# A state-space mixer rewritten on tiles of TensorE's array, with its transfers and table loads moved

## The chip, the cores and the metric

The kernel runs on one core of one Trainium2 chip. The metric is the device time of one execution in microseconds (us), given as the median of several runs. Everything below in lines L1, L2, ... refers to the kernel before, unless it is said to be of the change.

## The reference

Two transformer blocks are computed for 256 tokens of width 1024 in float32. The second one is: FFN, S5 mixer, FFN, FFN, block attention, FFN. Only the S5 mixer concerns the change:

```python
def s5_mixer(h, w_in, ..., d_skip, w_glu, w_out):
    u = (h @ w_in).astype(f32)
    ...
    # u in 64 groups of 16 values, per group a complex state of 64
    # st[t] = lam * st[t-1] + bb @ u[t];  y[t] = Re(c @ st[t])
    y = ys... + d_skip.astype(f32) * u
    g = jax.nn.gelu(y)
    g = g * jax.nn.sigmoid(g @ w_glu.astype(f32))
    return g.astype(h.dtype) @ w_out
```

The comment lines stand for the scan of the reference, which runs over the tokens of a chunk. A state is linear in the inputs, so the kernel may cut the 256 tokens into 32 chunks of 8: within a chunk, an output is a sum over taps (a Toeplitz matrix in time), and from chunk to chunk only the state is carried.

## The kernel before

**Weights.** A class `Stream` brings weights in units of 128x1024 (512 KB). `Stream._fill` issues each unit's DMA from SP (L61) into one of four buffers `raw` (eight in the FFN), then makes a high part `wh` on ScalarE (L74) and a rest `wl` on VectorE (L75), since each product of two float32 values is made of three matmuls in a faster format. `Stream.next` hands out the next pair and starts the work for units further ahead: a `raw` buffer is refilled when its unit has been split, a pair `wh`, `wl` (two are there, four in the FFN) when the matmuls that read it are done. `mode_a` (L320) makes one tile of 128 outputs by 256 tokens out of one unit, in 24 matmuls: for each of eight k, `wh` by `xh` (L325), `wh` by `xl` (L326), `wl` by `xh` (L327). `split` makes the high and low parts of activations (L257 on ScalarE, L258 on VectorE).

**Order.** A scheduler orders each engine's instructions. From `u_tile(6)` on, `manual_schedule` fixes that of TensorE and VectorE as written, up to `in_order.close()`. SP's queue and ScalarE's stay the scheduler's.

**FFN.** 22 chunks of the hidden width; each chunk takes three units (gate, up, down). The first one (`l == 0`) stands right ahead of the mixer.

**Mixer** (`s5_mixer`, L1172 on), with tables made long before by `s5_prep`: `lam` (powers of lambda), `cw` and `me` (the output and input maps of a chunk), `kr` (the taps), `pr`, `pi` (powers over chunks).
1. `tap_weights` (L1193) writes the taps of each tile into block-diagonal matrices `s5kb`: odd tiles on ScalarE, eight copies each; even ones on GpSimd (L1200), one multiply each.
2. `u_tile` (L1206), eight times: `mode_a`, a scale by the norm (L1212), a write to `u_dram` (L1214). After tiles 3 and 7, eight DMAs (L1219) bring `u` back as `s5us`, with time inside the chunk on the partitions.
3. `contribution` (L1235), twice: 64 matmuls `s5eps` (L1244) of 64 rows of output by 32 chunks, on tiles of the array, and copies to `s5e` (L1246).
4. `taps` (L1226), eight times: eight matmuls `s5yps` (L1231), and a copy.
5. `chunks` (L1248) is the recurrence over the chunks for half of the groups, on VectorE: two blocks of 16 chunks run side by side, so 16 turns of four instructions (L1261 to L1264); then four instructions of 480 values (L1274 on) carry the end of the first block into the second.
6. `spread` (L1286) writes states into a block-diagonal layout `s5sbd`; `states_out` (L1297) makes 16 matmuls `s5sps` (L1302) per quarter, copies (L1307) and writes `y_dram`, five DMAs of eight on SP, three on GpSimd (L1310). `states_in` (L1313) reads it back with features on the partitions.
7. Sum of taps and states (L1367), Gelu (L1368), split; then the GLU: `mode_a` with `s5gps`, Sigmoid (L1376), multiply, split; then the output projection.

Of the kernel before, what the change touches and what calls it, by code (L numbers as in the profile page):

```python
# [35 lines left out]
class Stream:  # L36
# [59 lines left out]
    def next(self):  # L96
        i = self.pos
        self.pos += 1
        self._fill(*(i + sum(n for _, n in pools) for pools in (self.raw_pools, self.hl_pools)))
        if self.units[i][2]:  # L100
            return self.parts.pop(i)
        return self.raws.pop(i)
# [25 lines left out]
class Net:  # L128
# [5 lines left out]
    def __init__(self, ctx, tc, i, out, tap=None):  # L134
# [18 lines left out]
        self.v_order = [*range(self.NLO, P), *range(self.NLO)]  # L153
        self.ada_late = list(range(5, 5 + 8 * 5, 5))
# [165 lines left out]
    def mode_a(self, ps, w, xh, xl):  # L320

        wh, wl = w
        for k in range(KT):
# [598 lines left out]
    def ffn(self, l, last_deep=None, out=None):  # L922
        nc, tc = self.nc, self.tc
        with tc.tile_pool(name=f"ffn{l}", bufs=2) as fp:
# [5 lines left out]
            prev = row = None  # L930
            for c in range(NFF):
                if c == last_deep:
                    self.stream.shallow()
# [66 lines left out]
    def s5_prep(self, lo, hi):  # L1000
# [169 lines left out]
        self.s5 = (lam, cw, me, kr, grp, pr, pi)  # L1170

    def s5_mixer(self):  # L1172
        nc, tc, i = self.nc, self.tc, self.i
        Q = 32
        lam, cw, me, kr, grp, pr, pi = self.s5
        with ExitStack() as st:
            wp = st.enter_context(tc.tile_pool(name="s5w", bufs=1))
            dp = st.enter_context(tc.tile_pool(name="s5d", bufs=1, space=bass.MemoryType.DRAM))
            u_dram = dp.tile([64, 16, 8, Q], F32, name="u_dram")
            y_dram = dp.tile([64, 16, 8, Q], F32, name="y_dram")  # L1180
            xh, xl = self.gained(self.cols[:, self.MIX_G : self.MIX_G + KT])
            rx = self.rstd()
            row = None
            l8 = wp.tile([P, 2, 2, Q], F32, name="s5l8")
# [4 lines left out]
            kbs = {}  # L1189

            uT = wp.tile([P, KT, 8, Q], F32, tag="sA", name="s5uT")
            us = wp.tile([P, 64, Q], F32, tag="sB", name="s5us")
            def tap_weights(f):  # L1193
                kb = wp.tile([P, 8, 8, 16], F32, tag="s5kb", name="s5kb", bufs=5)
                k = kr[:, f].rearrange("p (k n) -> p k n", n=16)
                if f % 2:
                    for g in range(8):
                        nc.scalar.activation(kb[:, :, g], k, AF.Copy, scale=grp[:, g : g + 1])
                else:
                    nc.gpsimd.tensor_mul(kb, k.unsqueeze(2).to_broadcast([P, 8, 8, 16]),  # L1200
                                         grp[:, 0:8].unsqueeze(1).unsqueeze(3).to_broadcast([P, 8, 8, 16]))
                kbs[f] = kb

            for f in (0, 2):
                tap_weights(f)
            def u_tile(f):  # L1206
                nonlocal row
                ps = self.pm.tile([P, S], F32, tag="m", name="s5ups")
                self.mode_a(ps, self.stream.next(), xh, xl)
                if row is None:  # L1210
                    row = self.rstd_row(wp, rx)
                nc.vector.tensor_mul(uT[:, f], ps.rearrange("p (c s) -> p s c", s=8),  # L1212
                                     row.rearrange("p (c s) -> p s c", s=8))
                nc.sync.dma_start(u_dram[8 * f : 8 * f + 8].rearrange("g n s c -> (g n) (s c)"),  # L1214
                                  uT[:, f].rearrange("p s c -> p (s c)"))
                if f % 4 == 3:
                    gs = slice(8 * f - 24, 8 * f + 8)
                    for s in range(8):
                        nc.sync.dma_start(us[16 * s : 16 * s + 16, gs], u_dram[gs, :, s].rearrange("g n c -> n g c"))  # L1219

            yc = wp.tile([P, KT, S], F32, name="s5yc")
# [3 lines left out]

            def taps(f):  # L1226

                kb = kbs.pop(f)
                ps = self.pm.tile([P, S], F32, tag="m", name="s5yps")
                for k in range(8):  # L1230
# [55 lines left out]
            def spread(hf):  # L1286
                for half in range(2):
# [4 lines left out]
                    else:  # L1292
                        nc.scalar.activation(sbd[hf][hs, :, :, half], src, AF.Copy)

            ys = []

            def states_out(qt):  # L1297

# [360 lines left out]
```

## Time and profile before

| | before |
|---|---|
| median of 3 runs | 2112.12 us (2111.94, 2112.12, 2116.03) |
| profiled execution, its own time | 2112.87 us |
| its span | 2111.1 us |
| TensorE busy (PE) | 2013.5 us, 95% |
| weight loads (PEld) | 1750.2 us, 83% |
| VectorE busy (DVE) | 1532.5 us, 73% |
| ScalarE busy (ACT) | 1057.0 us, 50% |
| GpSimd busy (POOL) | 472.3 us, 22% |
| HBM traffic | 178 GB/s over the span |
| mean granted clock of TensorE | 0.984 |

The span runs from the first instruction to the last of the profiled execution; the execution's own time has 1.8 us around it. A busy share is an average over all stages: the mixer is a short part (from about 1267 us to the end of the output projection near 1400), in which the shares differ from these. In the profile's timelines each row gives the start, the busy time, the engine, the line, the operation with its output and inputs, how many instructions the row holds, and in brackets the idle time of the engine just before and what ended it.

### The profile page before, as it was taken

How to read it: one execution, taken by the hardware profiler on the slowest of the kernel's cores; microseconds unless marked ns; L12 is line 12 of the kernel's file. 1: busy time of each engine (PE TensorE's matmuls, PEld its weight loads, DVE VectorE, ACT ScalarE, POOL GpSimd, SP SyncE). 2: the span in 40 equal slices, each digit the busy share in tenths (PEclk: the TensorE clock that was granted, in tenths of full speed). 3: DMA queues.
4: the chain of work that ended last, by engine and by line, in shares of the span. 5: the costliest groups of instructions: out<-in, count | busy, mean ns of one | idle time of the engine just before them, and what ended most of it. 6: DMA issues, size and time to landing. Idle time of an engine off the chain costs nothing. (4 is left out here: it accounts for less than half of the span.)

```text
span 2111.1 us, 33643 instructions
## 1 busy us (share of the span) xinstructions
PE 2013.5 (95%) x12222; PEld 1750.2 (83%) x12222; DVE 1532.5 (73%) x2986; ACT 1057.0 (50%) x1761; POOL 472.3 (22%) x506
## 2 busy tenths in 40 slices
PE   7998999999999899999999998899999999999999
PEld 5777999999999677788878888788887888777887
DVE  5867489878988666998776667566667666776666
ACT  4564544443444445555555544455555555565554
POOL 0000003028999232000031111101111111210111
PEclk9999999999999999999999999899999999999999
DMA  8773455554444776455555534355554555444552
GB/s 334 235 273 122 138 181 172 173 180 153 150 151 156 265 256 233 174 189 187 181 174 189 189 129 131 90 177 183 190 189 160 190 190 190 141 140 146 188 188 97
DMA packets 129623, 378.59 MB, mean 179 GB/s; under 512 B 26897, under 2 KB 41281, under 8 KB 129330
## 3 DMA queue, kind: packets, MB, share of 16 engines
q1 hardware_dynamic: 128448, 373.76, 52.5%
q0 software_dynamic: 1008, 2.69, 0.4%
q8 instruction: 96, 1.57, 0.3%
q14 instruction: 69, 0.57, 0.1%
q10 hardware_dynamic: 2, 0.00, 0.0%
HBM read 366.96 MB, written 9.44 MB: 178 GB/s over the span
## 5 line engine op out<-in xcount | busy, mean ns | idle before, releaser
L75 DVE TENSOR_TENSOR wl<-raw,wh 128x1024 fp32r<-128x1024 f32 (+1 forms) x595 | 743.1, 1251 | 372.1 <-ACT wh L74 368.6
L74 ACT ACTIVATE wh<-raw 128x1024 fp32r<-128x1024 f32 (+1 forms) x628 | 662.6, 1056 | 585.6 <-issue 316.6
L325 PE MATMUL ups<-xh,wh 128*128 128x256 f32 x1024 | 292.1, 285 | 0.3 <-ACT act_lo L803 0.2
L326 PE MATMUL ups<-xl,wh 128*128 128x256 f32 x1024 | 288.9, 282 | 0.0
L327 PE MATMUL ups<-xh,wl 128*128 128x256 f32 x1024 | 288.7, 282 | 0.0
L948 POOL TENSOR_TENSOR sgl<-sgl,rrow 128x256 f32<-128x256 f32 x88 | 126.1, 1433 | 718.1 <-ACT sgl L947 718.1
L335 PE MATMUL gps<-xx,wh 128*128 128x512 f32 x704 | 253.9, 398 | 6.6 <-DVE xx L314 6.6
L335 PE MATMUL upps<-xx,wh 128*128 128x512 f32 x704 | 251.0, 395 | 0.0
L343 PE MATMUL acc<-wh,gl 128*128 128x512 f32 x512 | 202.9, 398 | 6.4 <-DVE gl L258 6.2
L341 PE MATMUL acc<-wh,gh 128*128 128x512 f32 x512 | 202.3, 396 | 4.5 <-ACT gh L257 2.3
L727 POOL TENSOR_SCALAR ob<-iota,idxT 128x128 f32<-128x128 f32 x256 | 195.9, 783 | 34.8 <-PE ups L327 32.2
L336 PE MATMUL gps<-xx,wl 128*128 128x256 f32 x704 | 198.1, 281 | 0.5 <-DVE wl L75 0.5
L336 PE MATMUL upps<-xx,wl 128*128 128x256 f32 x704 | 197.7, 281 | 0.0
L325 PEld LDWEIGHTS ups<-xh,wh 128*128 128x128 f32 x1024 | 194.6, 190 | 0.9 <-ACT act_lo L803 0.8
L327 PEld LDWEIGHTS ups<-xh,wl 128*128 128x128 f32 x1024 | 193.8, 189 | 0.1
L326 PEld LDWEIGHTS ups<-xl,wh 128*128 128x128 f32 x1024 | 193.6, 189 | 0.1
L335 PEld LDWEIGHTS gps<-xx,wh 128*128 128x128 f32 x704 | 133.3, 189 | 38.1 <-DVE xx L314 7.8
L335 PEld LDWEIGHTS upps<-xx,wh 128*128 128x128 f32 x704 | 132.2, 188 | 30.8
L342 PE MATMUL acc<-wl,gh 128*128 128x512 f32 x380 | 150.8, 397 | 0.8 <-DVE wl L75 0.8
L341 PE MATMUL acc<-wh,hh 128*128 128x512 f32 x352 | 139.1, 395 | 6.6 <-ACT hh L257 6.5
L342 PE MATMUL acc<-wl,hh 128*128 128x512 f32 x352 | 138.3, 393 | 0.0
L336 PEld LDWEIGHTS gps<-xx,wl 128*128 128x128 f32 x704 | 133.5, 190 | 4.4 <-DVE wl L75 0.9
(406 smaller groups left out, 3691.9 us busy)
## 6 DMA issues: line engine op xcount, KB each, us to landing
raw<-peer_u SPq DMA_DIRECT2D x128, 512.0 KB, 3.3
raw<-peer_v SPq DMA_DIRECT2D x128, 512.0 KB, 3.3
raw<-ffn_gate SPq DMA_DIRECT2D x88, 512.0 KB, 3.2
raw<-ffn_up SPq DMA_DIRECT2D x88, 512.0 KB, 3.2
raw<-ffn_down SPq DMA_DIRECT2D x88, 512.0 KB, 3.2
raw<-w_ada SPq DMA_DIRECT2D x28, 512.0 KB, 4.5
raw<-w_in SPq DMA_DIRECT2D x24, 512.0 KB, 6.4
raw<-moba_w_qkv SPq DMA_DIRECT2D x24, 512.0 KB, 3.2
```

What stands on the lines that cost most here:

```text
L74: nc.scalar.activation(h[:, :n], raw[:, :n], AF.Copy)
L75: nc.vector.tensor_sub(lo[:, :n], raw[:, :n], h[:, :n].bitcast(F32))
L325: self.nc.tensor.matmul(ps, wh[:, s], xh[:, k], start=(k == 0), stop=False)
L326: self.nc.tensor.matmul(ps, wh[:, s], xl[:, k], start=False, stop=False)
L327: self.nc.tensor.matmul(ps, wl[:, s], xh[:, k], start=False, stop=(k == KT - 1))
L335: self.nc.tensor.matmul(ps, wh[:, s], xx[:, k], start=(k == 0), stop=False)
L336: self.nc.tensor.matmul(ps[:, 0], wl[:, s], xx[:, k, 0], start=False, stop=(k == KT - 1))
L341: mm(acc, lh, wh, start=start, stop=False)
L342: mm(acc, lh, wl, start=False, stop=False)
L343: mm(acc, ll, wh, start=False, stop=stop)
L727: nc.gpsimd.tensor_scalar(b, iota, idx[:, 1, n : n + 1], None, ALU.is_equal)
L948: nc.gpsimd.tensor_mul(sg, sg, row)
```

## The change

- **Taps as a Toeplitz table.** A DRAM tile `toep` takes, for each of eight tiles, one fill with zeros and eight writes of shifted taps: `toeplitz_out` issues these 72 DMAs on SP during chunks 2 to about 13 of the first FFN. `load_taps` brings four tiles of 512 KB at a time back to SBUF, twice in the mixer. The GpSimd and ScalarE work of `tap_weights` goes; eight small GpSimd copies make `s5pw`.
- **u.** The columns of `w_in` are permuted in the host's layout, so that a gather can go from SBUF to SBUF: eight DMAs each after tiles 3, 5 and 7, the last set half from SP's queue, half from ScalarE's. For tile 7, `next(ahead=False)` doesn't start the split of later weights.
- **Taps and states with tokens on the partitions.** Taps are 32 matmuls per half with `s5us` as the weight (a tile of 32 columns of the array), and states 64 matmuls per half on tiles of 64 rows by 32 columns, summed in the same PSUM. Gelu reads that PSUM; 32x32 turns on VectorE (`transpose`) bring features onto the partitions, so `y_dram`, the sum and the spreading are gone.
- **Recurrence** in four blocks of eight chunks: eight turns of twice the values, carries of three blocks by `s5pw`, and four instructions of 672 values.
- **Order.** `contribution(0)` and the first turns go between u tiles; `states_out(0)` stands inside the second recurrence; the first two GLU tiles do their matmuls in two halves of k. A Gelu and a Sigmoid of one element load the activation tables early.

```diff
+    def toeplitz_out(self, zero):
+        nc, kr = self.nc, self.s5[-1]
+        nc.gpsimd.memset(zero, 0.0)
+        for f in range(KT):
+            nc.sync.dma_start(self.toep[:, f].rearrange("p g k -> p (g k)"), zero)
+            for s in range(8):
+                nc.sync.dma_start(self.toep[16 * s : 16 * s + 16, f, :, 16 * s :].rearrange("n g k -> g n k"),
+                                    kr[:, f, : P - 16 * s])
+                if s % 3 == 2:
+                    yield
+            yield
...
             for c in range(NFF):
+                if 1 < c < NFF - 2:
+                    next(beside, None)
+                    next(beside, None)
...
+            def load_taps(hf):
+                toeplitz[hf] = wp.tile([P, 4, 8, P], F32, tag="s5tt", name="s5tt")
+                for f in range(4):
+                    nc.sync.dma_start(toeplitz[hf][:, f], self.toep[:, 4 * hf + f])
...
+            def gather(f0, f1):
+                for s in range(8):
+                    q = nc.scalar if f1 == KT and s % 2 else nc.sync
+                    q.dma_start(us[16 * s : 16 * s + 16, :, f0:f1].rearrange("p g f c -> p g (f c)"),
+                                uT[:, s, f0:f1].rearrange("p f c -> p (f c)"))
...
-                for c in range(16):
-                    n = 2 if c < 15 else 1
+                for c in range(8):
+                    n = 4 if c < 7 else 3
...
+                for b in (1, 2, 3):
+                    yield v.tensor_copy(sw[:, b - 1], s4[:, b, 0, ::-1])
+                    if b < 3:
+                        yield v.tensor_mul(t[:, 0], pw[:, hf, 0, 7], s4[:, b, 0])
+                        yield v.tensor_mul(t[:, 1], pw[:, hf, 1, 7], sw[:, b - 1])
+                        yield v.tensor_add(t[:, 0], t[:, 0], t[:, 1])
+                        yield v.tensor_add(s4[:, b + 1, 0], s4[:, b + 1, 0], t[:, 0])
...
+            def taps(hf):
+                for half in range(2):
+                    ps = yps[hf, half] = self.pa.tile([P, 4, P], F32, tag=f"acc{2 * hf + half}", name="s5yps")
+                    for f in range(4):
+                        for j in range(4):
+                            nc.tensor.matmul(ps[32 * j : 32 * j + 32, f], us[:, 2 * j + half, 4 * hf + f],
+                                             toeplitz[hf][:, f, 2 * j + half], start=(f == 0), stop=False,
+                                             tile_position=(0, 32 * j))
...
+            def states_out(hf):
...
+                                nc.tensor.matmul(yps[hf, half][32 * j : 32 * j + 32, f], ss[hf][hs, :, r, q % 16],
+                                                 cw[q // 8][hs, r, q % 8, 1:9].rearrange("p a b -> p (a b)"),
+                                                 start=False, stop=(f == 3 and r == 1), tile_position=(64 * half, 32 * j))
+                steps = []
+                for f0 in (0, 2):
+                    cs = slice(8 * f0, 8 * f0 + 16)
+                    for half in range(2):
+                        nc.scalar.activation(yg[:, cs, half], yps[hf, half][:, f0 : f0 + 2].rearrange(
+                            "p f (s n) -> p (f s) n", n=16), AF.Gelu_apprx_tanh)
+                    fs = slice(4 * hf + f0, 4 * hf + f0 + 2)
+                    def turn(fs=fs, cs=cs):
+                        nc.vector.transpose(yt[:, fs].rearrange("p f t -> p (f t)"), yg[:, cs].rearrange("p a b c -> p (a b c)"))
+                    steps += [turn, lambda fs=fs: self.split(gh[:, fs], gl[:, fs], yt[:, fs])]
+                return steps
...
+            u_tile(4)
+            u_tile(5)
+            gather(4, 6)
+            contribution(0)
+            run(rec0, 1)
+            run(rec1, 1)
+            run(rec0, 8)
             u_tile(6)
+            run(rec0, 8)
             u_tile(7)
+            gather(6, KT)
+            load = wp.tile([P, 2], F32, name="s5load")
             taps(0)
+            run(rec0, 99)
+            contribution(1)
+            nc.scalar.activation(load[:, 0:1], ee[1][:, 0, 0, 15:16], AF.Gelu_apprx_tanh)
+            load_taps(1)
+            run(rec1, 14)
...
+            steps = states_out(0)
             taps(1)
+            for step in steps:
+                step()
+                run(rec1, 4)
+            run(rec1, 99)
+            units = [self.stream.next()]
+            for step in states_out(1):
+                step()
+            nc.scalar.activation(load[:, 1:2], gh[:, KT - 1, 0:1].bitcast(F32), AF.Sigmoid)
+            units.append(self.stream.next())
...
+            for ks in (range(4), range(4, KT)):
+                for ps, w in first:
+                    self.mode_a(ps, w, gh, gl, ks)
             in_order.close()
```

**The order on SP in the first FFN.** `raw<-ffn_...` are the weight units; `toep_dram<-zero` is a fill, `toep_dram<-act_lo` a write of taps. Before:

```order
L61 DMA raw<-ffn_down 128x1024
L61 DMA raw<-ffn_gate 128x1024
L61 DMA raw<-ffn_up 128x1024
L61 DMA raw<-ffn_down 128x1024
L61 DMA raw<-ffn_gate 128x1024
```

After:

```order
L61 DMA raw<-ffn_gate 128x1024
L1185 DMA toep_dram<-zero 128x1024 x2
L61 DMA raw<-ffn_up 128x1024
L1187 DMA toep_dram<-act_lo 8x16x128
L1187 DMA toep_dram<-act_lo 8x16x112
L1187 DMA toep_dram<-act_lo 8x16x96
L1187 DMA toep_dram<-act_lo 8x16x80
L1187 DMA toep_dram<-act_lo 8x16x64
L1187 DMA toep_dram<-act_lo 8x16x48
L61 DMA raw<-ffn_down 128x1024
```

The weight units keep their order; up to six tap writes now stand between two of them in SP's queue.

**The order on VectorE where the first recurrence begins.** `s5uT` is a scaled u tile, `wl` the split of a weight unit, `s5t` and `s5s` the products and states of a turn. Before, with the last u tile scaled first:

```order
L1212 TENSOR_TENSOR s5uT<-s5ups,rrow 128x256
L1255 MEMSET s5s 128x2x32
L1261 TENSOR_TENSOR s5t<-s5l_13653,s5s 128x64
L1262 TENSOR_TENSOR s5t<-s5l_13653,s5s 128x64
L75 TENSOR_TENSOR wl<-raw,wh 128x1024
L1263 TENSOR_TENSOR s5t<-s5t,s5e_13665 128x64
L1264 TENSOR_TENSOR s5s<-s5t 128x2x32
```

After, from the second of two turns that follow the scale of tile 5:

```order
L1271 TENSOR_TENSOR s5t<-s5l_13726,s5s 128x128
L1272 TENSOR_TENSOR s5t<-s5l_13726,s5s 128x128
L1273 TENSOR_TENSOR s5t<-s5t,s5e_13742 128x128
L1274 TENSOR_TENSOR s5s<-s5t 128x4x32
L75 TENSOR_TENSOR wl<-raw,wh 128x1024
L1233 TENSOR_TENSOR s5uT<-s5ups,rrow 128x8x32
```

The split that here follows two turns is that of the weights of u tile 7, and the scale behind it that of tile 6.

**The order on TensorE from the last u tile to the GLU**, where `s5tt` are the Toeplitz taps and `act_lo` holds the maps. Here it stands for the change; before, `contribution` (L1244), the eight sets of taps (L1231) and the four of states (L1302) followed each other in the order of the calls at the end of the function above.

```order
L331 MATMUL s5ups<-xh,wl 128x256
L1302 MATMUL s5yps<-s5tt,s5us 32x128 x32
L1255 MATMUL s5eps<-s5us,act_lo 64x32 x64
L1315 MATMUL s5yps<-act_lo,s5s 32x128 x64
L1302 MATMUL s5yps<-s5tt,s5us 32x128 x32
L1315 MATMUL s5yps<-act_lo,s5s 32x128 x64
L329 MATMUL s5gps<-xh,wh 128x256
```

The first contribution now stands ahead of u tiles 6 and 7; the second set of taps stands behind the first states.

## Rows read from the trace of the kernel before

**Rows 1.** Table by stretch: us, busy time by engine, granted TensorE clock, DMA share, GB/s.
```profile
1130.00:1170.00 40.00, 40.00 (x212) 34.16 (x211) 26.39 (x39) 21.12 (x35) 7.38 (x5) 1.00 0.57 189
...
1310.00:1317.00 7.00, 6.32 (x129) 6.31 (x129) 3.92 (x24) 1.05 (x1) 0.00 (x0) 0.57 0.20 66
...
1357.00:1361.00 4.00, 3.66 (x19) 3.66 (x20) 2.25 (x7) 1.96 (x6) 0.00 (x0) 0.57 0.89 225
```

**Rows 2.** Timeline of TensorE in the mixer: start, busy us, operation, idle before.
```profile
1298.04 3.94 PE L1244 MATMUL s5eps<-s5us,act_lo 128*64 128x32 f32 x128
1301.92 4.79 PE L1231 MATMUL s5yps<-s5uT,s5kb 128*128 128x256 f32 x32
...
1310.68 6.35 PE L1244 MATMUL s5eps<-s5us,act_lo 128*64 128x32 f32 x128 [3.98 <-DMA s5us<-u_dram]
...
1357.34 0.79 PE L325 MATMUL s5gps<-xh,wh 128*128 128x256 f32 x2 [3.03 <-ACT xh L257]
...
1369.03 0.39 PE L325 MATMUL s5gps<-xh,wh 128*128 128x256 f32 x1 [1.94 <-ACT s5sg L1376]
```

**Rows 3.** Timeline of VectorE: scales of u, the recurrence, and what follows it.
```profile
1286.85 0.69 DVE L1212 TENSOR_TENSOR s5uT<-s5ups,rrow 128x256 f32<-128x256 f32 x1 [0.62 <-PE s5ups L327]
...
1292.50 0.70 DVE L1212 TENSOR_TENSOR s5uT<-s5ups,rrow 128x256 f32<-128x256 f32 x1 [0.63 <-PE s5ups L327]
...
1303.64 0.22 DVE L1261 TENSOR_TENSOR s5t<-s5l,s5s 128x64 f32<-128x64 f32 x1
...
1304.43 0.22 DVE L1261 TENSOR_TENSOR s5t<-s5l,s5s 128x64 f32<-128x64 f32 x1
...
1322.76 0.66 DVE L1274 TENSOR_TENSOR s5x<-act_lo,s5s 128x480 f32<-128x480 f32 x1
...
1350.21 0.76 DVE L1367 TENSOR_TENSOR s5yt<-s5yt,s5yc 128x256 f32<-128x256 f32 x2 [12.84 <-DMA s5yt<-y_dram]
```

**Rows 4.** Timeline of ScalarE: copies out of PSUM, spreading, the GLU's first tiles.
```profile
1302.03 1.06 ACT L1246 ACTIVATE s5e<-s5eps 128x512 f32<-128x512 f32 x1 [0.80 <-PE s5eps L1244]
...
1336.89 0.60 ACT L1307 ACTIVATE s5ys<-s5sps 128x512 f32<-128x512 f32 x1 [6.89 <-PE s5sps L1302]
...
1344.93 1.98 ACT L1293 ACTIVATE s5sbd<-s5s 64x1024 f32<-64x1024 f32 x1
...
1366.22 1.06 ACT L74 ACTIVATE wh<-raw 128x1024 fp32r<-128x1024 f32 x1 [0.97 <-PE s5gps L326]
1367.30 1.28 ACT L1376 ACT_TABLE_LOAD   x1
...
1373.07 0.36 ACT L1376 ACTIVATE s5sg<-s5gps 128x256 f32<-128x256 f32 x1
```

**Rows 5.** Transfers through DRAM, by tile: issue ns min/median/max, then landing us.
```profile
L1219 SPq DMA_DIRECT2D s5us<-u_dram x16: 322/486/3359, 1290.1 to 1307.9; - x16
L1214 SPq DMA_DIRECT2D u_dram<-s5uT x8: 319/326/1395, 1280.8 to 1298.8; - x8
...
DMA to landing us min/median/max: 2.5/3.1/5.7
...
L1310 SPq DMA_DIRECT2D y_dram<-s5ys x20: 303/450/879, 1337.5 to 1356.8; - x20
```

**Rows 6.** Timelines of VectorE and GpSimd where the mixer begins.
```profile
1269.15 2.94 DVE L75 TENSOR_TENSOR wl<-raw,wh 128x1024 fp32r<-128x1024 f32 x1
...
1279.03 1.22 DVE L75 TENSOR_TENSOR wl<-raw,wh 128x1024 fp32r<-128x1024 f32 x1
...
1265.27 5.75 POOL L1200 TENSOR_TENSOR s5kb<-act_lo 128x1024 f32<-128x1024 f32 x3 [4.65 <-PE acc L343]
```

**Rows 7.** TensorE in an earlier stage: matmuls of 32 columns, as a timeline row.
```profile
1067.11 3.77 PE L1150 MATMUL tps<-act_lo,gate_hi 128*32 128x128 f32 x128
```

**Rows 8.** Weight DMAs of the first FFN by line, 1090 to 1255 us; as rows 5.
```profile
L61 SPq DMA_DIRECT2D raw<-ffn_up x17: 327/328/328, 1092.7 to 1226.6; - x17
...
DMA to landing us min/median/max: 3.0/4.2/4.6
```

More of the change, by code (lines that the diff above doesn't have):

```diff
@@ L94, in skip, with next @@
         self.units = self.units[n:]
-    def next(self):
+    def next(self, ahead=True):
         i = self.pos
         self.pos += 1
-        self._fill(*(i + sum(n for _, n in pools) for pools in (self.raw_pools, self.hl_pools)))
+        raw, hl = (i + sum(n for _, n in pools) for pools in (self.raw_pools, self.hl_pools))
+        self._fill(raw, hl if ahead else i + 1)
         if self.units[i][2]:
@@ L153, in __init__ @@
         self.v_order = [*range(self.NLO, P), *range(self.NLO)]
+        dram = ctx.enter_context(tc.tile_pool(name="toep", bufs=1, space=bass.MemoryType.DRAM))
+        self.toep = dram.tile([P, KT, 8, P], F32, name="toep_dram")
         self.ada_late = list(range(5, 5 + 8 * 5, 5))
@@ L930, in ffn @@
             prev = row = None
+            beside = self.toeplitz_out(fp.tile([P, D], F32, name="zero", bufs=1)) if l == 0 else iter(())
             for c in range(NFF):
+                if 1 < c < NFF - 2:
+                    next(beside, None)
+                    next(beside, None)
                 if c == last_deep:
@@ L1188, in s5_mixer @@
             nc.vector.tensor_copy(l8[:, 1, 1], lam[:, 1, 8])
[L1189 to L1205, printed above, removed]
+            pw = wp.tile([P, 2, 2, 8, 2, 16], F32, name="s5pw")
+            for hf in range(2):
+                qs = slice(16 * hf, 16 * hf + 16)
+                for r in range(2):
+                    nc.gpsimd.tensor_copy(pw[:, hf, 0, :, r], pr[:, :8, qs])
+                    nc.gpsimd.tensor_copy(pw[:, hf, 1, :, r], pi[:, :8, r, qs])
+            uT = wp.tile([P, 8, KT, Q], F32, tag="sA", name="s5uT")
+            us = wp.tile([P, 8, KT, Q], F32, tag="sB", name="s5us")
             def u_tile(f):
@@ L1224, in s5_mixer @@
             ss = [both[:, hf] for hf in range(2)]
[L1226 to L1230, printed above, removed]
-                    nc.tensor.matmul(ps[:, k * Q :], kb[:, k].rearrange("p a b -> p (a b)"),
-                                     uT[:, f, 0 : 8 - k].rearrange("p s c -> p (s c)"), start=(k == 0), stop=(k == 7))
-                nc.scalar.activation(yc[:, f], ps, AF.Copy)
             def contribution(hf):
@@ L1329, in s5_mixer, with run @@
+            rec0, rec1 = chunks(0), chunks(1)
+            def run(rec, n):
+                for _ in range(n):
+                    next(rec, None)
+            for f in range(4):
                 u_tile(f)
-                if f in (1, 3):
-                    tap_weights(f)
-            for f in range(4, KT):
-                tap_weights(f)
+            gather(0, 4)
+            load_taps(0)
             in_order = ExitStack()
             in_order.enter_context(tc.manual_schedule(engines={mybir.EngineType.PE, mybir.EngineType.DVE}))
+            u_tile(4)
@@ L1362, in s5_mixer @@
+            units.append(self.stream.next())
+            oh = wp.tile([P, KT, S], F32R, tag="sB", name="s5oh")
+            ol = wp.tile([P, KT, S], F32R, tag="sS", name="s5ol")
+            first = [(self.pm.tile([P, S], F32, tag="m", name="s5gps"), w) for w in units]
+            for ks in (range(4), range(4, KT)):
+                for ps, w in first:
+                    self.mode_a(ps, w, gh, gl, ks)
             in_order.close()
-            self.tap("s5yc", yc)
-            gh, gl = self.xt_tiles()
@@ L1366, in s5_mixer @@
             for f in range(KT):
[L1367 to L1374 removed]
+                if f < 2:
+                    ps = first[f][0]
+                else:
+                    ps = self.pm.tile([P, S], F32, tag="m", name="s5gps")
+                    self.mode_a(ps, self.stream.next(), gh, gl)
```

146 lines of the change are left out of this document (37 added, 109 removed).

## The prediction

> **What bounds the kernel now.** I began with the table of stages. In the FFN ahead of the mixer TensorE is busy 40.00 of 40.00 us at full clock, while the DMA engines are at 0.57; nothing there but TensorE matters. Between 1298 and 1361 us it is different: the mean granted clock is 0.57 in the two later stretches shown, so mostly the lower of its two levels, 1.2 GHz [rows 1]. So I read the mixer's chain engine by engine.
>
> TensorE's order of time [rows 2] shows the projection u ending near 1298, then short bursts with waits: 3.98 us for the DMA that rearranges u, and 3.03 us for ScalarE before the GLU's matmuls, whose third tile starts at 1369.03. VectorE's order of time [rows 3] shows what fills that stretch: the recurrence over chunks from 1303 to 1337, then 12.84 us without work until states come back through DRAM. A table load of 1.28 us stands in ScalarE's queue right before a sigmoid that TensorE waits for [rows 4]. The stretch is thus one chain: rearrange u, contributions, recurrence, states out, DRAM and back, Gelu and split, GLU. The change rewrites this chain, so I price the new one and compare two marks that both kernels have: the fourth u tile scaled (1286.85 + 0.69 = 1287.5, [rows 3]) and the third GLU tile finished. A GLU or u tile has 24 matmuls and takes half of 1292.50 - 1286.85, that is 2.83 us [rows 3]; so the second mark is 1369.03 + 2.83 = 1371.9, and the stretch is 84.4 us long.
>
> **The new chain, step by step,** on the clock of the old trace.
>
> 1. The gather of u tiles 0 to 3 is eight DMAs from SBUF to SBUF. Its price isn't shown; the write of u to DRAM, with one run per partition too, takes 0.33 us to issue, the old gather 0.49; landing is 2.5 to 5.7, median 3.1 [rows 5]. I take 0.33 and 3.1: 1287.5 + 2.6 + 3.1 = 1293.2. TensorE ends u tile 5 at 1292.4 and so waits 0.8. The first contribution keeps its shape, 3.94 us [rows 2], to 1297.1; its second copy out takes 1.06 [rows 4]: 1298.3 with a hand-over.
> 2. VectorE: one step of the recurrence now takes eight instead of sixteen turns, on 128 instead of 64 values. A turn took 1304.43 - 1303.64 = 0.79 us; a value costs (0.66 - 0.22)/416 = 1.06 ns by the rows of 480 and 64 values [rows 3], so four instructions with 64 more cost 0.27: 1.06 a turn. Two turns (the first two multiplies done early) bring it to 1300.0; the split of u tile 7's weights, 1.22 us [rows 6], now stands behind them and holds that tile's third matmul until 1301.2, so TensorE ends u at 1303.8. Scale, two turns, scale: 1304.6. Four turns 4.2, the carries of the three later blocks (eleven instructions of 32 values) 2.1, four instructions of 672 values at 0.66 + 192 x 1.06 ns = 0.86, with hand-overs 3.5. The first recurrence ends at 1314.3. Taps, the last gather and the second contribution end by 1312 beside it. The old tap matmuls (four stretches, the first 4.79 us, [rows 2]) are gone, but for 64 small ones.
> 3. States out, first half: 64 matmuls on tiles of 64 rows by 32 columns. No row shows this form. The nearest, 128 rows by 32 columns with the same 128 moving columns, did 64 matmuls (128 records) in 3.77 us at full clock [rows 7]. TensorE has stood idle 2 to 3 us by then, and after such a wait the contribution took 6.35 instead of 3.94 [rows 2], at 0.57 of the clock [rows 1]; that would make 6.1. If eight tiles ran at once it would be 1.9. I take 4.5: 1318.8. Three Gelus of 256 columns, about 0.36 each [rows 4], spaced closer, 1.0: 1319.8.
> 4. VectorE then turns 512 columns, runs four recurrence instructions, splits, and so on. No row shows the turn; 480 values of an ordinary instruction cost 0.66, a strided copy of 64x1024 on ScalarE 1.98 [rows 3, 4]; it is one pass over the data, so I take 0.6. Two turns and two splits at 0.68 make 2.6, the sixteen recurrence instructions between them 4.2, the two left and the tail 6.0. The second recurrence ends at 1332.6. The DRAM copy of states, its 12.84 us wait, the spreading copies and the adds are all gone.
> 5. Second half: 4.5 for the matmuls, 1.0 for the Gelus, then turn, ScalarE copy (about 0.6, [rows 4]), split, twice in a row: 4.2. That is 1342.3. GLU tiles 0 and 1 did their first halves meanwhile; their second halves end near 1344.6. The weights of GLU tile 2 are split only when tile 0's are free (1343.2): 1.06 [rows 4] and 1.22 us [rows 6] later, at 1345.7 with hand-overs, its third matmul may go; it ends at 1348.3.
>
> The marks are 60.8 us apart instead of 84.4: **23.6 us less.** Both tables are now loaded beside other work; the second cost 1.28 us before [rows 4], inside these 23.6.
>
> **Ahead of the chain** GpSimd loses three multiplies of 5.75 us in all. VectorE's split beside one of them took 2.94 us, alone 1.22 [rows 6], and TensorE waits for that split. Eight small GpSimd copies take their place and ScalarE loses 16 tap copies. Bounds 0 and 4; I take 2.5.
>
> **In the first FFN** SP gets 8 zero fills and 64 tap writes over 12 chunks, each chunk 8.37 us (16 intervals of ffn_up from 1092.7 to 1226.6, [rows 8]): 100 us. Three weight loads a chunk issue in 0.33 each, 12 us; a tap write behind a fill waits up to 4.6 for it to land, 37 us for eight [rows 8]. 51 us are left for 72 issues, 0.71 each; writes to DRAM in small pieces took 0.30 to 0.88, median 0.45 [rows 5]. Besides, eight weight buffers are ahead, some 22 us of use. I cost it at nothing; TensorE's full 40.00 us covers it. If that cover goes, see rival 3. The two loads of taps (2 MB each) go beside the projection and the recurrence, with the DMA engines at 0.20 in the stretch 1310 to 1317 [rows 1].
>
> **The last gather on two queues:** at 0.33 to 0.49 an issue it saves 1.3 to 2.0 us, all of it beside the first recurrence, which ends some 2 us later; nothing in the sum. The Trainium skill, "DMA: Bandwidth & Descriptors", section "Issuing engines are not separate DMA queues", says that a second issuing engine saves only issue time and that both share the 16 DMA engines. By that rule the sum would be the same, since no issue time of this gather ends anything. No row here shows a transfer issued from ScalarE's queue.
>
> **Sum.** 2112.87 - 23.6 - 2.5 = 2086.8 for a profiled execution, which stood 0.75 above the median of 2112.12: **2086**. A measurement of this kernel tells some 0.2% (4.2 us) from no change.
>
> **Rivals.**
> 1. *Tiles side by side.* Forms of 64x32 leave room for eight matmuls at once. For: 64 of 128 columns one after the other would take some 17 us (16 tap matmuls of 144 columns on the mean took 4.79, [rows 2]); the form of 128x32 took 3.77 [rows 7], so about four ran at once, and half of that is 1.9. Against: the low clock after a wait. Sets of 1.9 instead of 4.5 give 5.2 more, 2081. The Trainium skill, "TensorEngine Tiling (Array Packing)", section "Tiling Modes", lists eight independent tiles for this shape and would have this rival; no row here shows that shape.
> 2. *A dear chain on VectorE and ScalarE.* Four turns at 1.98 instead of 0.6 add 5.5, two sets at 6.1 add 3.2, a gather landing in 5.7 adds 2.6: 2097. For: the longest landing did occur, and the low clock too.
> 3. *Weights late in the first FFN, slower than before.* SP issues in order, and weight loads now stand behind tap writes that each wait for the eighth DMA before them. With 22 us of buffers less 4.2 for landing, TensorE waits once 72 issues exceed 51 + 18 us, 0.96 each; the gain is lost at (69 + 26)/72 = 1.32, and at 1.45 the kernel is slower, 2121. Against: 0.88 was the longest such write [rows 5].
> 4. *The chain isn't what ends the stretch.* The split and GLU weights, or the taps from DRAM, come as late as before, and it stays within 0.2%: 2110. Against: weight loads are issued from freed buffers long before use, and ScalarE and VectorE have idle time in the old chain.
>
> **Chances.** Forecast 0.60; rival 1, 0.14; rival 2, 0.17; rival 3, 0.05; rival 4, 0.04. The low end takes rival 1 and an early gain of 4 with some tenths less for the turns (2086 - 5.2 - 1.5 - 1 = 2078), the high end rival 2: 2078 to 2098. Faster by over 0.2%: 0.91; within: 0.04; slower: 0.05.
>
> **What would show it.** Right: SBUF gathers landed by the end of u tile 5; VectorE without a wait over 2 us from the first recurrence to the second's end, about 34 us later; turns near 0.6; two bursts of states out at 3 to 6 us; the third GLU tile ending about 61 us after the fourth u tile was scaled; TensorE full in the first FFN. Wrong: TensorE waiting for weights in that FFN, turns of over 1 us, a wait for taps, or a table load between two Gelus.

## The result, and the profile after

The changed kernel takes 2083.33 us (median of four runs, 2082.09 to 2087.16), the kernel before 2112.03 in the runs beside it: a ratio of 0.9879, with a 95% interval of 0.9856 to 0.9902. The forecast was 2086, in a range of 2078 to 2098. The profiled execution took 2083.17 us with a span of 2081.4, against 2112.87 and 2111.1: 29.7 us less.

Where these 29.7 us lie is read from marks that both traces have. The first two are weight transfers, in the instructions of SP's line L61, by tile (count, issue time in ns, first and last start). Before:

```profile
L61 SPq DMA_DIRECT2D raw<-ffn_gate x88: 327/328/432, 1046.7 to 2067.8; - x88
L61 SPq DMA_DIRECT2D raw<-s_w_in x8: 327/328/333, 1251.7 to 1282.5; - x8
```

After:

```profile
L61 SPq DMA_DIRECT2D raw<-ffn_gate x88: 327/328/1289, 1043.7 to 2037.5; - x88
L61 SPq DMA_DIRECT2D raw<-s_w_in x8: 327/328/333, 1249.1 to 1276.0; - x8
```

The first FFN's first gate weights were issued 3.0 us earlier, in a part of the program that the change doesn't touch: in the profiles of this study that instant lies between 1041.0 and 1046.7. From there to the mixer's first weights it is 205.4 us against 205.0, so the first FFN gave 0.4 back. The rest is in the mixer. VectorE's order of time after (start, busy us, operation, in brackets the wait before and its releaser), which answers to [rows 3]:

```profile
1280.36 0.68 DVE L1233 TENSOR_TENSOR s5uT<-s5ups,rrow 128x256 f32<-128x256 f32 x1 [0.62 <-PE s5ups L331]
...
1294.96 0.29 DVE L1273 TENSOR_TENSOR s5t<-s5t,s5e 128x128 f32<-128x128 f32 x1 [7.67 <-ACT s5e L1257]
...
1309.76 0.86 DVE L1292 TENSOR_TENSOR s5s<-s5s,s5x 128x672 f32<-128x672 f32 x1
...
1314.11 0.70 DVE L1327 STREAM_TRANSPOSE s5yt<-s5yg 128x512 f32<-128x512 f32 x1
...
1325.73 0.86 DVE L1292 TENSOR_TENSOR s5s<-s5s,s5x 128x672 f32<-128x672 f32 x1
...
1331.35 0.71 DVE L1327 STREAM_TRANSPOSE s5yt<-s5yg 128x512 f32<-128x512 f32 x1 [2.50 <-ACT s5yg L1322]
...
1334.77 0.69 DVE L262 TENSOR_TENSOR xl<-s5yt,xh 128x512 fp32r<-128x512 f32 x1 [0.70 <-ACT xh L261]
```

The fourth u tile is scaled at 1281.04, which is 31.9 us after the mixer's first weights; before it was 35.8. The wait of 12.84 us for states from DRAM is gone; of the waits of over 2 us two are left, 7.67 us for the first contribution and 2.50 us for the second Gelus. What lies between the second recurrence's end and the third GLU tile shrank most. The last instruction of that recurrence before:

```profile
1335.57 0.66 DVE L1277 TENSOR_TENSOR s5s<-s5s,s5x 128x480 f32<-128x480 f32 x1
```

It ended 48.7 us after the fourth u tile was scaled, and 45.6 us after it in the change. TensorE's order of time after, which answers to [rows 2]:

```profile
1288.29 5.48 PE L1255 MATMUL s5eps<-s5us,act_lo 128*64 128x32 f32 x128 [2.32 <-DMA s5us<-s5uT]
...
1306.16 2.06 PE L1255 MATMUL s5eps<-s5us,act_lo 128*64 128x32 f32 x64 [1.67 <-DMA s5us<-s5uT]
1310.67 2.41 PE L1315 MATMUL s5yps<-act_lo,s5s 64*32 64x128 f32 x128 [2.45 <-DVE s5s L1292]
...
1326.64 3.63 PE L1315 MATMUL s5yps<-act_lo,s5s 64*32 64x128 f32 x128 [10.86 <-DVE s5s L1292]
...
1338.67 0.38 PE L331 MATMUL s5gps<-xh,wl 128*128 128x256 f32 x1 [0.49 <-DVE wl L75]
```

The last row is the third matmul of the third GLU tile; the 21 that follow it at 0.118 us end that tile at 1341.5. So the stretch between the two marks of the prediction is 60.5 us, against 84.4. Of the 23.9 us, 20.8 lie behind the second recurrence's end (35.7 before, 14.9 after), where the spreading, the way of the states through DRAM and the sum were, and 3.1 ahead of it. No run brings one of these back by itself, so their single shares are not shown. The table by stretch (columns as [rows 1]) shows TensorE full in the FFN beside tap writes, and what its clock did in the mixer:

```profile
1130.00:1170.00 40.00, 40.00 (x212) 34.17 (x211) 25.88 (x39) 21.33 (x35) 7.37 (x5) 1.00 0.80 249
1287.00:1295.00 8.00, 6.71 (x139) 6.70 (x140) 0.33 (x3) 2.18 (x2) 0.00 (x0) 0.79 0.31 83
1288.29:1293.77 5.48, 5.48 (x129) 5.44 (x129) 0.00 (x0) 1.06 (x1) 0.00 (x0) 0.69 0.21 45
1310.00:1316.00 6.00, 4.50 (x192) 3.79 (x192) 5.73 (x21) 2.66 (x7) 0.00 (x0) 1.00 0.53 215
1316.00:1326.00 10.00, 0.00 (x0) 0.00 (x0) 9.44 (x32) 0.63 (x1) 0.00 (x0) 0.69 0.01 2
1326.00:1331.00 5.00, 4.36 (x135) 4.04 (x136) 2.86 (x3) 0.61 (x3) 0.00 (x0) 0.59 0.44 121
```

The stretch from 1287 to 1295 reaches beyond the contribution, whose own 5.48 us are the row below it: its granted clock is 0.69, not 0.79. Two transfers by tile, the writes of taps in the FFN and the gathers of u, answer to [rows 5]:

```profile
L1187 SPq DMA_DIRECT2D toep_dram<-act_lo x64: 570/571/727, 1085.1 to 1175.3; - x64
...
L1239 SPq DMA_DIRECT2D s5us<-s5uT x20: 547/595/1597, 1281.1 to 1304.1; - x20
L1239 ACTq DMA_DIRECT2D s5us<-s5uT x4: 609/645/782, 1301.3 to 1303.5; - x4
```

The account of the profiled executions: 3.0 ahead of the change, -0.4 in the first FFN, 3.9 at the mixer's start, 23.9 between the marks, -0.7 behind the third GLU tile (739.2 us before, 739.9 after): 29.7.

### The profile page after: what moved, and what is told of

Read it like the earlier page. It is cut to its first block, busy times and chain, and to the rows that moved or that the text cites. A ratio compares the mean times of both kernels' runs of the same rounds, so it can differ in the third digit from the quotient of the medians.

```text
span 2081.4 us, 33810 instructions
## 1 busy us (share of the span) xinstructions
PE 1981.3 (95%) x12350; PEld 1717.5 (83%) x12350; DVE 1525.8 (73%) x2935; ACT 1037.0 (50%) x1712; POOL 456.5 (22%) x497
```

## The experiments

Single executions differ by some us ahead of the mixer, so the runs are compared by marks inside one execution: A, the first FFN (first gate weights to the mixer's first weights); B, from there to the end of the scale of the fourth u tile; C, from that to the issue of the last weights of the mixer's output projection, a mark that doesn't depend on how Gelu, Sigmoid and splits are ordered. S is the duration of the first set of states. Each row is one profiled execution.

| run | A | B | C | S |
|---|---|---|---|---|
| before | 205.0 | 35.8 | 107.9 | |
| the change | 205.4 | 31.9 | 83.8 | 2.41 |
| the change again | 205.1 | 31.9 | 85.3 | 3.70 |
| GpSimd multiplies back | 205.1 | 36.6 | 85.1 | 3.70 |
| last gather on one queue | 205.1 | 31.9 | 85.3 | 3.40 |
| first gather on two | 205.0 | 31.7 | 81.8 | 3.28 |
| tables not early | 206.4 | 31.9 | 86.4 | 3.71 |
| taps in one burst | 229.3 | 31.9 | 84.2 | 2.25 |
| split before turns | 204.9 | 31.9 | 84.5 | 3.68 |
| turns after | 206.8 | 31.9 | 83.1 | 2.40 |
| TensorE busy, first try | 205.3 | 31.9 | 93.6 | 3.40 |
| TensorE busy, second try | 205.5 | 31.9 | 82.3 | 2.24 |
| all together | 205.2 | 32.0 | 75.8 | 3.43 |
| all together, timed | 206.4 | 31.9 | 75.8 | 3.60 |

**The change again** is the unaltered kernel, timed beside the last run.

> The changed kernel once more, as the measure for the next run. It took 2083.33 us in four runs, so 2080 to 2087 is expected; a ratio to the kernel before of 0.985 to 0.990.

It took 2085.53 us (median of six, 2081.69 to 2091.36), a ratio of 0.9888 (0.9869 to 0.9907), which agrees with the first measurement; the difference of the medians is 24.7 us here and was 28.7 there. Its profile matters for all the others. TensorE's row for the first set of states:

```profile
1310.25 3.70 PE L1315 MATMUL s5yps<-act_lo,s5s 64*32 64x128 f32 x128 [2.45 <-DVE s5s L1292]
```

The same program, the same wait of 2.45 us, the same start to within half a us, and the set took 3.70 instead of 2.41. The table by stretch gives a granted clock of 0.50 for 1310 to 1316 (the lower level, 1.2 GHz) where it was 1.00. Everything behind it came 1.5 us later: C differs by that between two executions of one kernel. It isn't a matter of the chip: four of the runs below were made on one chip, and S was 2.25, 2.40, 3.40 and 3.68 in them. Hence a run is read beside the execution with the same S, and a difference in C of under 1.5 us with another S tells nothing. Two executions of one kernel are few for such a measure.

**GpSimd multiplies back.**

```diff
+            for f in range(3):
+                old = wp.tile([P, 8, 8, 16], F32, tag="s5x", name="s5old")
+                nc.gpsimd.tensor_mul(old, self.s5[-1][:, f]..., me[0][:, 0, 0, 0:8]...)
```

> The changed kernel plus three GpSimd multiplies of 128x1024 at the start of the mixer, of the form that the change took away; their result is used by nothing. From the first GpSimd copy of the mixer (1262.70 in the changed kernel) to the end of the scale of the fourth u tile it takes 18.3 us in the changed kernel, and from the first GpSimd multiply (1265.27) 22.3 us before. Theory: VectorE's splits run long beside GpSimd's multiplies and TensorE waits for them, so the stretch grows by 2.5 to 4.5 us and a split of some 2.9 us appears again. Rival: the gain came from ScalarE's missing tap copies or from the order of transfers; then the stretch grows by less than 1 us.

B grew by 4.6 us, a little above the expected range, and from the first GpSimd copy to the scale it was 23.0 instead of 18.3. The expected long split didn't appear: it began 0.04 us ahead of the second multiply and took 1.21 us, and that multiply took 2.96 us instead of 1.93. Other instructions of VectorE ran long. GpSimd and VectorE in its timelines:

```profile
1262.59 6.98 POOL L1226 TENSOR_TENSOR s5old<-act_lo 128x1024 f32<-128x1024 f32 x3
...
1263.01 1.54 DVE L1214 TENSOR_SCALAR s5l<-act_lo 128x32 f32<-128x32 f32 x1
...
1266.47 1.10 DVE L285 TENSOR_TENSOR s<-ss 128x2 f32<-128x2 f32 x1
...
1267.81 1.78 DVE L243 TENSOR_SCALAR rs_i<-rs_w 128x2 int32<-128x2 int32 x1
```

Instructions of 2 and 32 values, 0.17 us elsewhere in the same listing, took 1.10 to 1.78 while GpSimd multiplied, each of the three until within 0.05 us of the end of a multiply, and none after 1269.6. So the gain at the start is the removal of these multiplies; ScalarE's tap copies, still absent in this run, are not needed to explain it.

**Last gather on one queue.**

```diff
-                    q = nc.scalar if f1 == KT and s % 2 else nc.sync
+                    q = nc.sync
```

> The last gather of u (tiles 6 and 7) on SP's queue alone, as the other two. An issue took 0.6 us on SP in the changed kernel, so eight in a row end about 1.4 to 2 us later than the two sets of four did. Theory of the prediction: beside the first recurrence this costs nothing; the third GLU tile ends within 0.5 us of 60.0 us after the fourth u tile was scaled. Rival: the second contribution waited 1.67 us for this gather already, its copy ended 1309.3 and the second recurrence asked for it at 1310.9, so 1.6 us of cover is too little and the second recurrence starts up to 1 us later.

TensorE waited 3.28 us for this gather instead of 1.67, and the second half of the contribution then took 3.63 us at the low clock instead of 2.06. C is 1.6 above the change's first profile and equal to that of its repeat, whose S is like the one here. The rival's delay did come: the second recurrence's first addition stood 31.5 us after the fourth u tile instead of 29.9. In the repeat, where it stood at 30.1, VectorE then waited 1.18 us for a Gelu, so its chain was as late. So the second queue of the last set is worth between nothing and 1.6 us in this order; more runs of both would be needed to say which.

**First gather on two queues.**

```diff
-                    q = nc.scalar if f1 == KT and s % 2 else nc.sync
+                    q = nc.scalar if f1 != 6 and s % 2 else nc.sync
```

> The first gather (tiles 0 to 3) issued half from SP's queue, half from ScalarE's, as the last one is. In the changed kernel its eight issues took 0.6 us each and it landed 7.2 us after the scale, TensorE waited 2.32 us for it and then ran the contribution in 5.48 us at a granted clock of 0.79. Theory: the issue bounds the landing; it comes 2 to 2.4 us earlier, the wait goes, the contribution takes nearer to 3.9, and the first recurrence begins 3 to 4 us earlier; the third GLU tile ends 2.5 to 4 us sooner after the fourth u tile. Rival: the landing is bound by what the 16 DMA engines move and not by the issues; then it moves by less than 0.5 us. A second one: ScalarE's copies of weights are held up behind its four issues and the gain is given back.

TensorE's timeline:

```profile
1287.12 3.93 PE L1255 MATMUL s5eps<-s5us,act_lo 128*64 128x32 f32 x128 [0.59 <-DMA s5us<-s5uT]
```

The gather landed 5.3 us after the scale instead of 7.2, the wait fell to 0.59 us, and the contribution ran at the full clock in 3.93: the first recurrence began 3.5 us earlier, as expected. In each of the ten profiles with this gather on one queue TensorE waited 2.25 to 2.96 us for it, and the contribution took 5.35 to 5.84. C gained 2.0 against the first profile and 3.5 against the repeat, whose S is nearer. In this run the last gather held TensorE for 3.44 us and bounded what came next.

**Tables not early.**

```diff
-            nc.scalar.activation(load[:, 0:1], ee[1][:, 0, 0, 15:16], AF.Gelu_apprx_tanh)
...
-            nc.scalar.activation(load[:, 1:2], gh[:, KT - 1, 0:1].bitcast(F32), AF.Sigmoid)
```

> The two one-element activations that load the Gelu and the Sigmoid table early are left out. Theory: each load of 1.28 us then stands right before the first Gelu and the first Sigmoid. The Gelu's delays the turn on VectorE by about 1.3 us at most, since the states came out at 1313.1 and VectorE asked for the turn at 1314.1; the Sigmoid's falls beside matmuls of GLU tiles 1 and 2. So the third GLU tile ends 0.5 to 2.5 us later than 60.0 us after the fourth u tile. Rival: both are covered, and nothing moves by more than 0.3 us.

ScalarE's timeline shows both loads back on the path, and TensorE's the wait that follows the second:

```profile
1315.50 1.28 ACT L1322 ACT_TABLE_LOAD   x1 [4.79 <-PE s5yps L1315]
1316.80 1.21 ACT L1322 ACTIVATE s5yg<-s5yps 128x256 f32<-128x256 f32 x4
...
1340.79 1.28 ACT L1387 ACT_TABLE_LOAD   x1
...
1342.53 0.38 PE L329 MATMUL s5gps<-xh,wh 128*128 128x256 f32 x1 [1.32 <-ACT s5sg L1387]
```

C is 2.7 above the first profile and 1.2 above the repeat, whose S is the same: 1.2 to 2.7 us for both loads.

**Taps in one burst.**

```diff
-                    next(beside, None)
-                    next(beside, None)
+                    for _ in range(99):
+                        next(beside, None)
```

> All 72 issues that write the Toeplitz taps stand together in chunk 2 of the first FFN, not six a chunk. An issue took 0.57 us in the changed kernel, so the burst takes 41 us of SP's queue. Theory: the weight buffers cover some 18 us (eight units of 2.8 us less 4.2 us for landing), and TensorE waits for the rest: 15 to 25 us in that FFN, and the kernel is slower than the one before less 26 us by as much. Rival: the issues don't hold up weight loads, since the scheduler spreads them or since what is queued ahead lasts longer; then the FFN takes within 2 us of 202.5 us (first ffn_gate issue 1043.7 to first w_in issue of the mixer 1249.1: 205.4).

The first FFN took 229.3 us, 23.9 more. In the table by stretch of this run TensorE falls to 6.24 of 20 us:

```profile
1090.00:1110.00 20.00, 20.00 (x107) 17.07 (x106) 10.48 (x18) 7.31 (x13) 3.33 (x3) 1.00 0.43 132
1110.00:1130.00 20.00, 6.24 (x20) 4.48 (x18) 2.07 (x3) 1.86 (x3) 0.72 (x1) 0.57 0.44 129
1130.00:1150.00 20.00, 15.84 (x66) 12.57 (x66) 11.48 (x15) 10.30 (x14) 1.48 (x1) 0.83 0.98 381
```

The kernel took 2107.93 us against 2107.21 for the kernel before: without the spreading of the writes over 12 chunks, this one execution shows nearly the whole gain lost.

**Split before turns.**

```diff
             gather(4, 6)
+            w6 = self.stream.next()
             contribution(0)
...
-            u_tile(6)
+            u_tile(6, w6)
```

> The low part of u tile 7's weights is made on VectorE ahead of the first turns of the recurrence, in the 7.67 us that VectorE waits there, and not behind two turns. Theory: TensorE's wait of 0.80 us for it goes and the recurrence loses 1.14 us of foreign work; the first recurrence ends 1.0 to 1.3 us earlier, as does the third GLU tile against the fourth u tile. Rival: the second contribution (copied by 1309.3) then bounds the second recurrence, and less than 0.5 us comes through to the GLU.

The gather landed 0.7 us later than in the change, and still the first recurrence ended 0.5 to 0.7 us earlier. C is 0.8 below the repeat, whose S is the same (3.7), and 0.7 above the first profile, whose S isn't. The expected 1.0 to 1.3 was missed, and the rival's bound appeared: the second contribution was copied 29.8 us after the fourth u tile, and the second recurrence's first addition came at 29.9, no earlier than in the change. It is a small gain, of the size of what single executions leave open.

**Turns after.**

```diff
-            for step in steps:
-                step()
-                run(rec1, 4)
             run(rec1, 99)
             units = [self.stream.next()]
-            for step in states_out(1):
+            for step in steps + states_out(1):
```

> The two turns and two splits of the first half (0.70 and 0.68 us) stand behind the second recurrence instead of inside it. Theory: the second recurrence ends 2.7 us earlier; the four stand in VectorE's wait of 2.50 us for the second Gelus, which now is partly filled; the third GLU tile ends 1.5 to 2.5 us earlier. Rival: the GLU's first halves are then held up, TensorE waits there for as long, and it ends within 0.5 us of the 60.0.

The second recurrence ended 2.3 us earlier, but C fell by only 0.7 at the same S. ScalarE ran the second half's Gelus behind the first half's splits, at 1331.33, although TensorE had the states at 1329.6, and VectorE alternated between a turn, 0.70 us of wait for ScalarE, and a split. Most of the gain became this new wait.

**TensorE kept busy, two tries.**

```diff
             taps(1)
+            idle = self.pm.tile([P, S], F32, tag="m", name="s5idle")
+            for k in range(72):
+                nc.tensor.matmul(idle, xh[:, 0, :P], xl[:, k % KT], start=True, stop=True)
```

> 72 matmuls of 256 columns whose result nothing reads fill most of the 10.86 us in which TensorE waits for the second recurrence. In the changed kernel the granted clock falls from 1.00 to 0.59 after that wait, and 64 matmuls of states take 3.63 us where the first set took 2.41. Theory: with the wait filled the clock stays at 1.00 and the second set takes 2.3 to 2.5; the third GLU tile ends 1.0 to 1.4 us earlier. Rival: the set is bound by something other than the clock, and stays at 3.4 to 3.7.

C rose by 9.8 us: the added matmuls read the buffers that the first half's splits write, so ScalarE, which writes the high part there, waited 9.54 us for them, and VectorE 8.71 us for ScalarE. The try says nothing of the clock. The second one reads other buffers:

```diff
             taps(1)
+            idle = self.pm.tile([P, S], F32, tag="m", name="s5idle")
+            for k in range(36):
+                nc.tensor.matmul(idle[:, :P], self.ident, us[:, k % 8, 0:4].rearrange("p f c -> p (f c)"), start=True, stop=True)
```

> The same question as with the 72 matmuls, which turned out to hold up the first half's splits: they read the buffers xh, xl that the splits write. Now 36 matmuls of 128 columns in full float32 from other buffers (the identity and the gathered u), whose result nothing reads, fill TensorE's wait of 10.86 us. Theory: the second set of states takes 2.3 to 2.5 us instead of 3.63, VectorE's chain ends its second recurrence as before at 45.5 us after the fourth u tile, and the turn after it comes 1.0 to 1.4 us earlier than at 50.31. Rival: the set stays at 3.4 to 3.7 us.

TensorE's timeline and the table by stretch of this run:

```profile
1313.83 8.31 PE L1368 MATMUL s5idle<-s5us,ident 128*128 128x128 f32 x72
1324.11 2.23 PE L1315 MATMUL s5yps<-act_lo,s5s 64*32 64x128 f32 x128 [1.97 <-DVE s5s L1292]
```

```profile
1324.00:1328.00 4.00, 3.89 (x142) 3.73 (x143) 3.03 (x4) 1.21 (x4) 0.00 (x0) 1.00 0.42 137
```

The second set took 2.23 us at full clock instead of 3.63, the turn behind it came at 48.9 instead of 50.3 us, and C fell by 1.5. So the clock is what bound that set.

**All together.** The steps above that helped, with turns and splits reordered (both turns, then both splits) and the last gather on three queues:

```diff
-                    q = nc.scalar if f1 == KT and s % 2 else nc.sync
+                    q = (nc.sync, nc.scalar, nc.gpsimd)[s % 3] if f1 == KT else nc.scalar if f0 == 0 and s % 2 else nc.sync
...
+                    if hf and b:
+                        fill(8)
...
-                return steps
+                return steps[0::2] + steps[1::2]
...
+            fill(32)
```

> The changed kernel with what the runs so far point to: the first gather on two queues; the last on three (SP, ScalarE, GpSimd); the split of u tile 7's weights ahead of the turns; the first half's turns behind the second recurrence, and in each half both turns ahead of both splits; matmuls that nothing reads ahead of the last contribution and in the wait for the second recurrence. By the single runs: the first recurrence starts 3.5 us earlier and takes 1.1 less; with the last gather landing in time the second ends 2.75 us earlier still, at 38 to 40 us after the fourth u tile instead of 45.55; the GLU's first two tiles gain 1 us more by the order of turns and splits. Theory: the third GLU tile comes 6 to 8.5 us earlier. Rival: the last gather lands no earlier than before, and the second recurrence ends at 41 to 43 us; the gain is 3 to 5 us.

VectorE's timeline:

```profile
1317.10 0.86 DVE L1294 TENSOR_TENSOR s5s<-s5s,s5x 128x672 f32<-128x672 f32 x1
1317.88 2.35 DVE L75 TENSOR_TENSOR wl<-raw,wh 128x1024 fp32r<-128x1024 f32 x2
1320.15 1.30 DVE L1329 STREAM_TRANSPOSE s5yt<-s5yg 128x512 f32<-128x512 f32 x2
1321.55 1.29 DVE L262 TENSOR_TENSOR xl<-s5yt,xh 128x512 fp32r<-128x512 f32 x2
1322.96 1.30 DVE L1329 STREAM_TRANSPOSE s5yt<-s5yg 128x512 f32<-128x512 f32 x2
1324.38 1.29 DVE L262 TENSOR_TENSOR xl<-s5yt,xh 128x512 fp32r<-128x512 f32 x2
```

The second recurrence ended 38.6 us after the fourth u tile instead of 45.6, and from there VectorE ran turns and splits in pairs with waits of 0.1 us. C is 75.8, 8.0 less than in the change's first profile and 9.5 less than in its repeat, whose S is nearer. One step did not do its part: the matmuls ahead of the last contribution kept that at full clock (2.07 us), but after a wait of 1.68 us the first set still took 3.43, and 3.60 in the profile of the timed run. The second set, behind the filled wait, took 2.24 and 2.23. Timed:

> The kernel with all the steps together, unaltered, timed. Its third GLU tile came 8.0 us earlier after the fourth u tile than in the changed kernel (sigmoid at 53.45 instead of 61.44 us). Theory: the stages behind the mixer take as long as before, so the 8 us reach the total: 2073 to 2077 us, 0.3 to 0.5% under the changed kernel of the same call. Rival: the gain is given back behind the GLU, and the two lie within 0.2%.

It took 2074.31 us (median of five, 2070.14 to 2077.44), a ratio to the kernel before of 0.9831 (0.9814 to 0.9849); the change in the same call took 2085.53, with an interval of 0.9869 to 0.9907 that doesn't touch this one. That is 11.2 us or 0.54% under the change, somewhat more than expected; in the two profiles of that call C differs by 9.5. This version beats both kernels.

## Why the prediction was right

**The stages.** The table of stages said that only the mixer mattered, and the account above bears it out: 27.8 us came between the mixer's first weights and the third GLU tile, 0.4 was given back in the FFN and 0.7 behind.

**The chain between the marks.** Forecast 60.8 us, measured 60.5. Most of the saving came where the chain had it: 20.8 us behind the second recurrence's end, where the forecast makes 20.0 (35.7 less 15.7). That the whole came within 0.3 us is luck, since two errors of some 3 us cancelled. Measured from the fourth u tile, with the forecast in brackets: gather landed 7.2 (5.7), first contribution ended 12.7 (9.6), first recurrence ended 29.6 (26.8), first turn begun 33.1 (32.3), second recurrence ended 45.6 (45.1), last split 54.4 (54.8). The first part was under-priced. The step "I take 0.33 and 3.1" for the gather failed: its issues took 0.6 us each on SP, and the run with two queues shows that the issue bounded the landing. With it failed "the first contribution keeps its shape, 3.94 us": TensorE waited 2.3 us, not 0.8, and the contribution took 5.48 at a mean clock of 0.69. With the wait cut to 0.59 it took 3.93 again at 1.00.

The second part was over-priced. "I take 4.5" for a set of states measured 2.41 and 3.63, and 2.24 in the run where the clock was full. The form of 64x32 is faster than that of 128x32 [rows 7] by 3.77 / 2.24 = 1.7 times, so at that clock rival 1 with its 1.9 had the better price. At the lower clock, which the prediction held against it, a set took 3.6 to 3.7, and 4.5 was nearer. Rival 1's time was not reached since the first part lost 2.8 us. The 32x32 turn, taken at 0.6, took 0.70; the long instructions and the turns of the recurrence were as worked out (0.86 for 672 values, 1.06 for a turn of the recurrence). Of the prediction's own signs of being right two failed: the gather landed 2.3 us after u tile 5, and the first set of states took 2.41 us, not 3 to 6. The others held or nearly.

**The start.** 2.5 was taken, 3.9 measured, inside its bounds of 0 and 4; the run with the multiplies back shows the cause, and the way that the prediction gave stands in TensorE's timelines before and after:

```profile
1272.15 0.58 PE L327 MATMUL s5ups<-xh,wl 128*128 128x256 f32 x1 [3.49 <-DVE wl L75]
```

```profile
1266.47 0.38 PE L331 MATMUL s5ups<-xh,wl 128*128 128x256 f32 x1 [0.49 <-DVE wl L75]
```

TensorE's wait for the split fell by 3.0 us, most of the 3.9.

**The first FFN.** Costed at nothing; 0.4 measured, within what the other profiles of the change's FFN show (204.9 to 206.8). Each write took 0.57 us against the limit of 0.96 that rival 3 gave, and SP waited for fills to land 8.9 us in all, in six waits, not 37; the burst shows that the rival's mechanism is real and what it costs once the cover is used up.

**The last gather.** "Nothing in the sum" is not refuted: the run with one queue left between nothing and 1.6 us. The reason given, two us of slack behind the second contribution, was right in the trace (1.6 us between its copy and its use). With one queue the second half of the contribution began 1.6 us later, less than the 2.4 us of four issues; in the change one of SP's four issues had waited 1.0 us for an earlier DMA of this gather to land. The Trainium skill, "DMA: Bandwidth & Descriptors", section "Issuing engines are not separate DMA queues", allows a second queue the issue time alone. The trace agrees: the first gather on two queues landed 1.9 us earlier, less than the four issues of 0.6 us that left SP's queue. But that time stood on the path and brought the clock with it, 3.5 us by the start of the recurrence; the last gather's did not clearly.

**The tables.** Counted with 1.28 for the second; both together cost 1.2 to 2.7 when not loaded early.

**Rival 4** didn't come about: GLU weights held TensorE up for 0.49 us at the third GLU tile, and the second taps, with a pause of 0.60 us whose end the profile doesn't name, were done 10.86 us before the states that TensorE waited for.

Of the 28.7 us between the medians, 26.7 lie from the first FFN on in the two profiles; the other 3.0 of the profiled 29.7 came from the part ahead, which differs from one execution to the next. With the repeat's C, 1.5 us longer, they would be about 25, and its own call gave 24.7 between the medians.

## What to carry to other kernels

In a short chain of waits, price a DMA set by its number of issues and look for an idle queue that can take half. Cutting a wait gave back the wait and also sped up the work behind it, where TensorE's granted clock then stayed at 1.00. Where the wait can't be cut, matmuls that nothing reads can hold the clock, if they read no buffer that anyone waits to write: they did in the long wait of three profiles, but ahead of the last contribution they did not help the first set. And compare experiments by marks within one execution, after one repeat of the same kernel has shown how far those marks move by themselves.

## What the runs showed of the hardware that was not expected

- The same kernel with the same wait of 2.45 us ran the same 64 matmuls once at a granted clock of 1.00 in 2.41 us and once at 0.50 in 3.70.
- A DMA between SBUF and SBUF mostly took 0.55 to 0.65 us of its queue, on SP, ScalarE and GpSimd alike, whether it moved two tiles or four; a 512 KB weight load took 0.33.
- Beside GpSimd's multiplies, VectorE instructions of two values took up to 1.78 us instead of 0.17, and ended with a multiply.
- A turn of 128x512 in 32x32 blocks took 0.70 us on VectorE, about as long as a subtraction of the same size (0.68).
